# A two-layer hybrid encoder on one core: plain token tiles in the last output projection, and the memory keys' fetch and the gates' exchange moved

## The chip, the core and the metric

The kernel runs on one core of one Trainium2 chip. The metric is the device time of one execution in microseconds. The core has a matrix engine (TensorE, PE in the profile, with its weight loads as PEld), a vector engine (VectorE, DVE), an activation engine (ScalarE, ACT), GpSimd (POOL) and a queue engine (SyncE, SP). Each runs its own list of instructions in order; semaphores hold an instruction until what it needs is done. Transfers are issued by SP and POOL and carried by sixteen DMA engines.

## The reference: what is computed

There are 512 tokens of width 2048 and two layers, all in float32. A layer normalises its input, multiplies it with one input projection of 4,928 columns, and splits the result into latents for attention, three blocks for a short gated convolution, queries for the memory, and gates:

```python
h = rmsnorm(x, pre_norm_g[l])
z = h @ w_in[l]
q_lat, kv_lat, k_pe, gb, gc, xin, q_mem, gate = split_cols(z)
# group A: latent attention, 8 heads of 192, rotary part of 64, softmax over all 512 tokens
# group B: gb * conv3(gc * xin) along the tokens
# group C: attention of 4 heads of 128 into 256 memory tokens
y = jnp.concatenate([a_out, c_out, m_out], axis=-1) * jax.nn.silu(gate)
o = y @ w_o[l]
x = x + rmsnorm(o, post_norm_g[l])
```

The rotary tables come from the token positions, and the memory tokens are normalised and projected to keys and values in every layer.

## The kernel before

**Products.** TensorE multiplies float32 numbers as two parts each: a high part rounded to `fp32r` and the low rest. Each product is three matmuls (`mm3`, L272 to L274): high by high, high by low, low by high. ScalarE makes the high part of a weight tile (L189, `wh`), VectorE the low part (L190, `wl`). The large products go by Strassen's scheme: seven products `P1` to `P7` of half-size blocks instead of eight, in a `group` of passes. The function `ended` adds finished products into the output tiles, and sums of weight blocks are formed by accumulating transfers that POOL issues (L146, `wr`).

**Stages of a layer.** The input projection runs as five groups. The fifth makes the attention's gates `ga0` and `ga1`; between its steps stand turns of the latents and of the memory queries (`more`). Then `mixer` runs: the rotary part of the queries (`q_rope_steps`: products `qr` on TensorE, then a rotation on VectorE, L1067 to L1077, with a table `tab` that is fetched from DRAM, split and written back to DRAM and reloaded as `QR`), then sixteen steps of the four memory heads, then eight attention heads with the first pass of the output projection mixed in. A step of a head is a score product `sc`, its negated row maximum `nm` on VectorE (L1182), an exponential on ScalarE (L1185), a reciprocal `rec` (L1187), a scaling (L1188), a transposition `ptp` on TensorE (L1198), its split into `PT` (L277, L278), and a product `o` with the values, which is multiplied by the gates in `y` (L1213). Last comes `out_proj`: two groups of 1024 columns, each finished token tile squared and summed (L1346), multiplied with the gain (L1350) and added to the residual `xr` (L1395).

**Token order.** The host gives x in an order in which each tile of 128 tokens takes 32 from each quarter of a 128-token block; 32 x 32 transposes on VectorE (L933) and sixteen small transfers (`exchange`, L941) then bring the gates into rows by channel, `y`, with tokens in plain order. The output projection takes its left operand from `y`. With `Left(False, True)` (argument `apart`) the splits reorder the tokens back into the host's tiles, so that the result's tile t holds tokens 32t to 32t+31 of each of the four blocks of 128. The final store is therefore a view of four pieces of 32 rows.

**What sets the order.** The program is a list of steps. TensorE, SP and POOL follow it as written; what a step defers (`pr.defer`) is issued as room comes. VectorE and ScalarE are ordered by a scheduler with its own estimate of when data arrive. Tiles come from pools with a fixed number of buffers: 8 `raw`, 19 `slabs`, 8 PSUM banks. The last group of the last layer keeps the weights of its last product in tiles of their own (`hold`: `T4h` and `T4l`) and runs it as one step, one token half after the other.

Of the kernel before, what the change touches and what calls it, by code (L numbers as in the profile page):

```python
# [12 lines left out]
P = 128  # L13
# [3 lines left out]
NT = S // P  # L17
# [68 lines left out]
class Program:  # L86
# [23 lines left out]
    def add(self, fn, units=(), room=0.0, ahead=None):  # L110

        self.steps.append((list(units), fn, room, self.ahead if ahead is None else ahead))
# [115 lines left out]
def encoder(tc, x, xt, mem, memt, positions, columns, w_in, q_norm_g, w_uq, w_qr, kv_norm_g, w_ukv,  # L228
# [3 lines left out]
    nc = tc.nc  # L232
    depth = w_in.shape[0]
# [15 lines left out]
    add = pr.add  # L249
# [11 lines left out]
    def slab(name, dt=F32):  # L261
        return slabs.tile([P, D], dt, tag="slab", name=nm(name))
# [680 lines left out]
    def gate_rows(k, name, C):  # L943
        def f():
            pr.until(lambda: C.get((name, "turned")) == NT)
            exchange(y_slab(k), C[name])
        return f
# [314 lines left out]
    def mixer(l, C, pair2, tail):  # L1262

        add(tables_fetch)
        add(mem_fetch)
        (p0, rotate0, fetch0), (p1, rotate1, fetch1) = (q_rope_steps(l, g) for g in range(2))
        add(gate_rows(1, "ga1", C))
        put(p0)
        add(gate_rows(0, "ga0", C))
        put(rotate0)  # L1270
        sts = [{} for _ in range(4)]
        qkv = qkv_steps(l, 0, sts[0])
        qkv[0] += (0.0, 1)
        qkv[2] += (0.0, 0)
        put(qkv[:1])
        its = [it for i in range(4) for it in mem_head(i)]
        m = len(its)
        between = {k: [s] for k, s in zip((2, 5, 8, 10, 12), qkv[1:])}
        between.setdefault(6, []).append((fetch0, []))
        between[m - 2] = [(lambda: pr.prep_next(), [])]  # L1280
        for pair in range(4):
            for i in range(2):
                its += mla_head(2 * pair + i, sts[pair])
            nxt = tail if pair == 3 else spread(8, qkv_steps(l, pair + 1, sts[pair + 1]))
            if pair == 0:
                nxt = dict(zip((-1, 1, 3, 4, 6, 7), nxt_steps(nxt)))
            if pair == 2:
                nxt.update(pair2)
            for k, v in nxt.items():
                between.setdefault(m + 8 * pair + k, []).extend(v)  # L1290
        late = [(4, (tables_fetch, [])), (5, p1[0]), (6, p1[1])] + list(zip((6, 7, 8, 9), rotate1)) + [(11, (fetch1, []))]
        if l + 1 < depth:
            late += zip((12, 14, 16, 17, 18, 19, 20, 21), mem_turned_steps(l + 1))
        for k, s in late:
            between.setdefault(m + k, []).append(s)
        pipeline(its, between, m)


    def y_half(k, h):
        return G["ys"][k].rearrange("q c (p k) -> q (c p) k", k=P)[:, :, 64 * h:64 * h + 64]  # L1300

    def out_proj(l):
        last = l == depth - 1
        st = {"n": [0] * NT, "og": {}, "ssq": {}}

        def og(t):
            if t not in st["og"]:
                st["og"][t] = slab("og")
                st["ssq"][t] = small(4, f"ssqo{t}")
            return st["og"][t]  # L1310

        def gains(g):
            def f():
                for j in range(2):
                    st["g", g, j] = scrap("g2")
                    (nc.sync if g else nc.gpsimd).dma_start(st["g", g, j], post_norm_g[l, (2 * g + j) * 512:(2 * g + j + 1) * 512]
                                        .partition_broadcast(P))
            return f

        def block(g):  # L1320
            def f(h, j, c):
                r = h * 1024 + c * 256
                k = (2 * g + j) * 512
                return w_o[l, r:r + 256, k:k + 512].rearrange("(a p) c -> p a c", p=P)
            return f

        def slot(g):
            return lambda i, j, tt: og(2 * i + tt)[:, (2 * g + j) * 512:(2 * g + j + 1) * 512]

        def factor(t):  # L1330
            if last and t == NT - 1:
                st["r", t] = rsqrt_mean(st["ssq"][t][:, 2:3], D, more=st["pre"], on=nc.vector)
            else:
                tot = small(1, "tot2")
                nc.vector.tensor_reduce(tot, st["ssq"][t], axis=AX.X, op=ALU.add)
                st["r", t] = rsqrt_mean(tot, D, on=nc.vector)

        def fin(g):
            def f(i, j, tt, ps=None):
                t, k = 2 * i + tt, 2 * g + j  # L1340
                cs = slice(k * 512, (k + 1) * 512)

                def scale():
                    o = st["og"][t][:, cs]
                    src = o if ps is None else ps
                    nc.scalar.activation(G["junk"], src, AF.Square, accum_out=st["ssq"][t][:, k:k + 1])  # L1346
                    st["n"][t] += 1
                    if st["n"][t] == 4:
                        factor(t)
                    nc.vector.tensor_tensor(o, src, st["g", g, j], op=ALU.mult)  # L1350
                    if last and t == NT - 1 and st["n"][t] == 3:
                        sums = st["ssq"][t]
                        pre = st["pre"] = small(1, "pre")
                        nc.vector.tensor_reduce(pre, sums[:, :2], axis=AX.X, op=ALU.add)
                        nc.vector.tensor_tensor(pre, pre, sums[:, 3:], op=ALU.add)
                        nc.vector.tensor_scalar(pre, pre, 1.0 / D, EPS, op0=ALU.mult, op1=ALU.add)
                    if st["n"][t] == 4:
                        residual(l, st, t)
                if ps is None:
                    pr.defer(0.7, scale)  # L1360
                else:
                    if last and g == 1:
                        pr.until(lambda: st["n"][t] == 3)
                    scale()
            return f

        def fetch(t):
            def f():
                st.setdefault("x", {})[t] = slab("xr")
                nc.gpsimd.dma_start(st["x"][t], G["src"][t * P:(t + 1) * P, :])  # L1370
            return f

        hold_n = [0]

        def hold():
            if hold_n[0] % 2 == 0:
                st["hold"] = slab("T4h", F32R), slab("T4l", F32R)
            k = hold_n[0] % 2
            hold_n[0] += 1
            return tuple(t[:, k * 1024:(k + 1) * 1024] for t in st["hold"])  # L1380

        g0 = group(G["left"], ("o", l, 0), 512, block(0), slot(0), SECOND, fin(0), direct=fin(0))
        g1 = group(G["left"], ("o", l, 1), 512, block(1), slot(1), LATE, fin(1), hold if last else None,
                   direct=fin(1))
        return g0, g1, gains, fetch

    def residual(l, st, t):
# [4 lines left out]
        def part(c, n=1024):  # L1392
            cs = slice(c, c + n)
            xt = st["x"][t]
            nc.vector.scalar_tensor_tensor(xt[:, cs], og[:, cs], st["r", t], xt[:, cs], op0=ALU.mult, op1=ALU.add)  # L1395
            if last:
                nc.sync.dma_start(out[0].rearrange("(p t j) c -> t p j c", t=NT, j=32)[t][:, :, cs], xt[:, cs])
            else:
                nc.gpsimd.dma_start(G["dst"][rows, cs], xt[:, cs])

# [35 lines left out]
    def put(*passes):  # L1436
        for steps in passes:
            for s in steps:
                add(*s)

    def weave(steps, extra, every, n=1):

        out, extra = [], list(extra)
        for k, s in enumerate(steps):
            out.append(s)
            if (k + 1) % every == 0:
                out += extra[:n]
                extra = extra[n:]
        return out + extra
# [10 lines left out]
    for l in range(depth):  # L1460
# [128 lines left out]
        put(g4[13:16])  # L1589
        lat = [latent_turn(l, "cq", j) for j in range(4)] + [latent_turn(l, "ckv", j) for j in range(2)] + [k_rope_turn]  # L1590
        more = [(f, []) for f in lat + [qm_turn(j, C) for j in range(4)]]
        put(weave(g4[16:], more, 2, 2))
        G["left"] = Y = Left(False, True)
        g0, g1, gains, fetch = out_proj(l)

        def low(p):
            return lambda: G["left"].split("A12", p, y_half(2 + p, 0))

        def use_y(Y=Y):
            G["left"] = Y  # L1600

        def sums(p):
            def f():
                a11, a12, a21, a22 = (y_half(k, h) for h in range(2) for k in (p, 2 + p))
                left = G["left"]
                pr.defer(1.2, lambda: left.split("A11", p, a11))
                pr.defer(1.2, lambda: left.split("A22", p, a22))
                combine(left, p, a11, a12, a21, a22)
            return f
# [66 lines left out]
```

## Time and profile before

| what | us |
|---|---|
| median of 3 runs | 1497.22 (1497.14 to 1498.55) |
| profiled execution, its own time | 1496.37 |
| its span, first to last instruction | 1494.5 |
| TensorE busy | 1453.4 (97%) |
| VectorE busy | 1096.8 (73%) |
| ScalarE busy | 871.7 (58%) |
| POOL busy | 270.0 (18%) |
| mean granted TensorE clock | 0.988 |

All times in views of the profile count from the span's start. A row of the timeline has start, duration, engine, line and operation, the tile written `<-` the tiles read, a count where equal rows are merged, and in brackets the idle time just before it with the instruction that ended it. Matmuls overlap: one of 128x512 is listed with 0.39 us, though the next starts 0.23 us later. A DMA row has 16 engines as its whole: a share of 25% is four engines' worth.

### The profile page before, as it was taken

The page shows a single profiled execution, that of the slowest core. Times are in us where ns is not written, and L with a number is a line of the kernel's source. Part 1 is how long each engine was busy: PE and PEld are TensorE (multiplying, and loading weights), DVE is VectorE, ACT ScalarE, POOL GpSimd, SP SyncE. Part 2 cuts the span into 40 slices and gives each one's busy share as a digit, 9 for nine tenths or more (in the row PEclk, how much of TensorE's full clock was granted, in tenths as well). Part 3 has the DMA queues.
Part 4 walks back from the last instruction along what each step waited for, and adds up shares of the span by engine and source line. Part 5 has one row for each costly group of instructions (what it writes and reads, how often), then busy time and mean ns, then how long its engine had stood idle before and what let it go on. Part 6 is the DMA issues. An engine that isn't in the chain of part 4 may idle for free.

```text
span 1494.5 us, 19452 instructions
## 1 busy us (share of the span) xinstructions
PE 1453.4 (97%) x7104; PEld 1239.8 (83%) x7104; DVE 1096.8 (73%) x1461; ACT 871.7 (58%) x1328; POOL 270.0 (18%) x276
## 2 busy tenths in 40 slices
PE   9999999999999999999999999999999999999991
PEld 8887888898878888888898888889988788888881
DVE  5899676957668788878979566766677776877872
ACT  7855345446568787554886334544555767865540
POOL 0031303032201100312201431121131100023010
PEclk9999999999999999999999999999999999999995
DMA  9999979697976462996978999787988915249562
GB/s 358 403 267 217 220 200 178 157 214 203 233 202 147 120 232 74 169 253 159 326 261 256 222 244 215 180 180 169 222 202 199 240 63 118 67 100 188 177 175 93
DMA packets 156348, 295.21 MB, mean 198 GB/s; under 512 B 11292, under 2 KB 46620, under 8 KB 152412
## 3 DMA queue, kind: packets, MB, share of 16 engines
q0 software_dynamic: 56576, 129.51, 43.0%
q1 hardware_dynamic: 99676, 164.45, 34.8%
q8 instruction: 56, 0.92, 0.3%
q14 instruction: 40, 0.33, 0.1%
HBM read 266.01 MB, written 21.63 MB: 192 GB/s over the span
## 4 chain that ended last, share of the span: by engine, by line
PE 94%; DMA 2%; ACT 1%; DVE 1%; SPq 0%; issue 0%; POOLq 0%; DVEq 0%; ACTq 0%
PE P L272 23%; PE P L273 23%; PE P L274 23%; PE ptp L1198 2%; PE o L273 1%; PE o L272 1%; PE o L274 1%; PE sc L274 1%; PE sc L272 1%; PE sc L273 1%; PE tps L915 1%; PE sc L1179 1%; PE qps L272 1%; PE qps L274 1%; PE qps L273 1%; PE sc L1180 1%
## 5 line engine op out<-in xcount | busy, mean ns | idle before, releaser
L190 DVE TENSOR_TENSOR wl<-wr,wh 128x1024 fp32r<-128x1024 f32 (+2 forms) x436 | 515.8, 1187 | 264.1 <-ACT wh L189 260.4
L189 ACT CAST wh<-wr 128x1024 fp32r<-128x1024 f32 (+2 forms) x436 | 444.6, 1023 | 442.6 <-PE P L274 342.3
L272 PE MATMUL P<-wh,S 128*128 128x512 f32 (+1 forms) x896 | 345.1, 385 | 0.0
L273 PE MATMUL P<-wl,S 128*128 128x512 f32 (+1 forms) x896 | 343.7, 384 | 0.0
L274 PE MATMUL P<-wh,S 128*128 128x512 f32 (+1 forms) x896 | 343.2, 383 | 0.0
L272 PE MATMUL P<-wh,A 128*128 128x512 f32 (+1 forms) x656 | 253.0, 386 | 0.0
L273 PE MATMUL P<-wl,A 128*128 128x512 f32 (+1 forms) x656 | 251.8, 384 | 1.1 <-DVE wl L190 1.1
L274 PE MATMUL P<-wh,A 128*128 128x512 f32 (+1 forms) x656 | 251.5, 383 | 0.0
L146 POOL DMA_DIRECT2D wr<-in_w_in_dram x132 | 158.3, 1200 | 444.1 <-DVE wl L190 264.0
L274 PEld LDWEIGHTS P<-wh,S 128*128 128x128 f32 x896 | 168.2, 188 | 30.5
L273 PEld LDWEIGHTS P<-wl,S 128*128 128x128 f32 x896 | 168.2, 188 | 29.5
L272 PEld LDWEIGHTS P<-wh,S 128*128 128x128 f32 x896 | 168.1, 188 | 29.5
L273 PEld LDWEIGHTS P<-wl,A 128*128 128x128 f32 x656 | 123.2, 188 | 23.4 <-DVE wl L190 1.9
L274 PEld LDWEIGHTS P<-wh,A 128*128 128x128 f32 x656 | 123.1, 188 | 22.4
L272 PEld LDWEIGHTS P<-wh,A 128*128 128x128 f32 x656 | 123.1, 188 | 21.7 <-ACT og L586 0.2
L146 POOL DMA_DIRECT2D wr<-in_w_o_dram x40 | 48.4, 1248 | 298.0 <-DVE wl L190 292.9
L1185 ACT ACTIVATE P<-sc,nm 128x512 f32<-128x512 f32 (+1 forms) x96 | 59.4, 619 | 34.9 <-DVE nm L1182 34.5
L1188 ACT ACTIVATE P<-P,rec 128x512 f32<-128x512 f32 (+1 forms) x96 | 62.2, 656 | 5.9 <-DVE rec L1187 5.8
L1182 DVE TENSOR_REDUCE nm<-sc 128x1 f32<-128x512 f32 (+1 forms) x96 | 56.8, 595 | 11.8 <-PE sc L274 6.3
L1198 PE MATMUL ptp<-identr,P 128*128 128x128 f32 x320 | 46.9, 275 | 0.8 <-ACT P L1188 0.8
L178 DVE TENSOR_TENSOR wr<-wr,wr 128x1024 f32<-128x1024 f32 (+1 forms) x36 | 42.2, 1175 | 5.6 <-DMA wr<-in_w_in_dram 5.1
L1198 PEld LDWEIGHTS ptp<-identr,P 128*128 128x128 f32 x320 | 38.5, 142 | 7.4 <-ACT P L1188 1.3
(318 smaller groups left out, 2077.0 us busy)
## 6 DMA issues: line engine op xcount, KB each, us to landing
wr<-in_w_in_dram SPq DMA_DIRECT2D x128, 512.0 KB
wr<-in_w_in_dram POOLq DMA_DIRECT2D x108, 512.0 KB, 7.5
wr<-in_w_o_dram SPq DMA_DIRECT2D x48, 512.0 KB
wr<-in_w_o_dram POOLq DMA_DIRECT2D x40, 512.0 KB, 7.2
wr<-in_w_in_dram SPq DMA_DIRECT2D x32, 416.0 KB
wr<-in_w_in_dram POOLq DMA_DIRECT2D x24, 416.0 KB, 5.9
wr<-in_w_mk_dram SPq DMA_DIRECT2D x15, 512.0 KB
wr<-in_w_mv_dram SPq DMA_DIRECT2D x15, 512.0 KB
```

What stands on the lines that cost most here:

```text
L146: engine.dma_start(dst, src, **kw)
L178: nc.vector.tensor_tensor(tiles[a], tiles[a], tiles[b], op=ALU.add)
L189: pin(nc.scalar.copy(hi[:, h], src[:, h]))
L190: pin(nc.vector.tensor_tensor(lo[:, h], src[:, h], hi[:, h].bitcast(F32), op=ALU.subtract))
L272: nc.tensor.matmul(ps, ah, bh, start=first, stop=False, **kw)
L273: nc.tensor.matmul(ps, ah, bl, start=False, stop=False, **kw)
L274: nc.tensor.matmul(ps, al, bh, start=False, stop=last, **kw)
L915: nc.tensor.transpose(ps[:, t * P:(t + 1) * P], v[:, 4 * j:4 * j + 4].rearrange("p g j -> p (g j)") if len(v.shape) == 3 else v[:, j * P:( ...
L1182: nc.vector.tensor_reduce(nmax, ps, axis=AX.X, op=ALU.max, negate=True)
L1185: nc.scalar.activation(pt, ps, AF.Exp, bias=nmax, accum_out=tot)
L1188: nc.scalar.activation(pt, pt, AF.Copy, scale=rec)
L1198: nc.tensor.transpose(ps[:, k * P:(k + 1) * P], pt[:, k * P:(k + 1) * P], G["ident"])
```

## The change

There are three edits.

In the last layer the output projection no longer reorders its tokens. `Left` is made with `apart` false, `y_half` gives columns 256h to 256h+255 of each channel block as they lie, and the splits are plain. The result's tile t then holds tokens 128t to 128t+127; the residual for it is collected from the tiled DRAM buffer by four transfers of 32 rows each instead of one of 128, and the store goes to 128 consecutive rows.

In both layers `mem_fetch`, which reloads the memory keys `Km` and values `Vm` (1 MB each) from DRAM, is moved from the start of `mixer` to just before the last two entries of the projection's list, the last weight step and the last turn of the memory queries. It now stands ahead of `tables_fetch`.

In both layers the two exchanges of gates are moved from around the `qr` products to steps 2 (`ga0`) and 12 (`ga1`) of the memory heads.

```diff
     def mixer(l, C, pair2, tail):
         add(tables_fetch)
-        add(mem_fetch)
         (p0, rotate0, fetch0), (p1, rotate1, fetch1) = (q_rope_steps(l, g) for g in range(2))
-        add(gate_rows(1, "ga1", C))
-        put(p0)
-        add(gate_rows(0, "ga0", C))
-        put(rotate0)
+        put(p0, rotate0)
...
         between = {k: [s] for k, s in zip((2, 5, 8, 10, 12), qkv[1:])}
+        between.setdefault(2, []).append((gate_rows(0, "ga0", C), []))
         between.setdefault(6, []).append((fetch0, []))
+        between.setdefault(12, []).append((gate_rows(1, "ga1", C), []))
...
-    def y_half(k, h):
+    def y_half(l, k, h):
+        if l == depth - 1:
+            return G["ys"][k][:, :, 256 * h:256 * h + 256]
         return G["ys"][k].rearrange("q c (p k) -> q (c p) k", k=P)[:, :, 64 * h:64 * h + 64]
...
         def fetch(t):
             def f():
-                st.setdefault("x", {})[t] = slab("xr")
-                nc.gpsimd.dma_start(st["x"][t], G["src"][t * P:(t + 1) * P, :])
+                x = st.setdefault("x", {})[t] = slab("xr")
+                if last:
+                    for i in range(NT):
+                        nc.gpsimd.dma_start(x[32 * i:32 * i + 32], G["src"][P * i + 32 * t:P * i + 32 * t + 32, :])
+                else:
+                    nc.gpsimd.dma_start(x, G["src"][t * P:(t + 1) * P, :])
...
             if last:
-                nc.sync.dma_start(out[0].rearrange("(p t j) c -> t p j c", t=NT, j=32)[t][:, :, cs], xt[:, cs])
+                nc.sync.dma_start(out[0][rows, cs], xt[:, cs])
...
-        put(weave(g4[16:], more, 2, 2))
-        G["left"] = Y = Left(False, True)
+        put(weave(g4[16:], more, 2, 2)[:-2])
+        add(mem_fetch)
+        put(weave(g4[16:], more, 2, 2)[-2:])
+        G["left"] = Y = Left(False, l + 1 < depth)
```

The list of TensorE's instructions is the same before and after. Three other lists move where the prediction looks.

ScalarE at the end of the last layer, before (the product P7 has two token halves, `P_1182` and `P_1183`; `T4h` are the high parts of the last product's weights):

```order
L189 CAST wh_12752<-B_1184_12445 128x1024
L189 CAST T4h_12756<-wr_12256 128x1024
L189 CAST T4h_12756<-wr_12274 128x1024
L189 CAST T4h_12776<-wr_12292 128x1024
L189 CAST T4h_12776<-wr_12310 128x1024
L586 COPY og_11668<-P_1182_12415 128x512
L586 COPY og_11679<-P_1183_12416 128x512
L1346 ACTIVATE junk,ssqo_1123_11669<-og_11668 128x512
```

The same place on ScalarE now:

```order
L189 CAST wh_12764<-B_1184_12445 128x1024
L586 COPY og_11668<-P_1182_12415 128x512
L1346 ACTIVATE junk,ssqo_1123_11669<-og_11668 128x512
L586 COPY og_11679<-P_1183_12416 128x512
L189 CAST T4h_12768<-wr_12256 128x1024
L189 CAST T4h_12768<-wr_12274 128x1024
L189 CAST T4h_12788<-wr_12292 128x1024
L189 CAST T4h_12788<-wr_12310 128x1024
```

VectorE at that place now, from its last `wl` on (`T4l` are the low parts of the same weights):

```order
L190 TENSOR_TENSOR wl_12765<-B_1184_12445,wh_12764 128x1024
L587 SCALAR_TENSOR_TENSOR og_11668<-og_11668 128x512
L1350 TENSOR_TENSOR og_11668<-og_11668,g_1186_12466 128x512
L587 SCALAR_TENSOR_TENSOR og_11679<-og_11679 128x512
L1399 SCALAR_TENSOR_TENSOR xr_12553<-og_11666,r_12748,xr_12553 128x1024
L190 TENSOR_TENSOR T4l_12769<-wr_12256,T4h_12768 128x1024
L190 TENSOR_TENSOR T4l_12769<-wr_12274,T4h_12768 128x1024
L190 TENSOR_TENSOR T4l_12789<-wr_12292,T4h_12788 128x1024
L1399 SCALAR_TENSOR_TENSOR xr_12553<-og_11666,r_12748,xr_12553 128x1024
L190 TENSOR_TENSOR T4l_12789<-wr_12310,T4h_12788 128x1024
```

Both copies of P7 and a square now stand ahead of the four casts; in before the casts stood ahead of them, and the four `T4l` stood ahead of both L587.

VectorE at the start of the memory heads of layer 1, before (`rm` and `qr` belong to the rotation, `nm` are the maxima of the memory heads):

```order
L190 TENSOR_TENSOR wl_10142<-wr_9950,wh_10141 128x1024
L190 TENSOR_TENSOR wl_10545<-wr_9968,wh_10544 128x1024
L1182 TENSOR_REDUCE nm_10222<-sc_10218 128x1
L1182 TENSOR_REDUCE nm_10234<-sc_10230 128x1
L1182 TENSOR_REDUCE nm_10246<-sc_10242 128x1
L1187 RECIPROCAL rec_10227<-tot_10225 128x1
L1187 RECIPROCAL rec_10239<-tot_10237 128x1
L1182 TENSOR_REDUCE nm_10273<-sc_10269 128x1
L1187 RECIPROCAL rec_10251<-tot_10249 128x1
L1067 TENSOR_TENSOR rm_10188<-qr_10145,tab_10115 128x1024
```

The same place now:

```order
L190 TENSOR_TENSOR wl_10125<-wr_9950,wh_10124 128x1024
L1067 TENSOR_TENSOR rm_10154<-qr_10128,tab_10119 128x1024
L1071 TENSOR_TENSOR qr_10128<-qr_10141,tab_10119 128x512
L1072 TENSOR_TENSOR qr_10141<-qr_10141,tab_10119 128x512
L1077 TENSOR_TENSOR rm_10154<-rm_10154,qr_10128 128x512
L1076 TENSOR_TENSOR rm_10154<-rm_10154,qr_10141 128x512
L190 TENSOR_TENSOR wl_10545<-wr_9968,wh_10544 128x1024
L278 TENSOR_TENSOR Q_10168<-qps_10169,Q_10168 128x512
L278 TENSOR_TENSOR rm_10154<-rm_10154,qrh_10160 128x1024
L1182 TENSOR_REDUCE nm_10188<-sc_10184 128x1
L1182 TENSOR_REDUCE nm_10200<-sc_10196 128x1
L1182 TENSOR_REDUCE nm_10212<-sc_10208 128x1
```

The whole rotation has moved ahead of the first maximum; it stood behind the fourth.

SP's last stores, before (the sizes are those of the side that is written):

```order
L1397 DMA out_dram<-xr_12553 4x32x1024 x2
L1397 DMA out_dram<-xr_12607 4x32x1024 x2
L1397 DMA out_dram<-xr_12661 4x32x1024 x2
L1397 DMA out_dram<-xr_12750 4x32x256 x2
L1397 DMA out_dram<-xr_12750 4x32x512 x3
```

The same stores now:

```order
L1401 DMA out_dram<-xr_12553 128x1024 x2
L1401 DMA out_dram<-xr_12610 128x1024 x2
L1401 DMA out_dram<-xr_12667 128x1024 x2
L1401 DMA out_dram<-xr_12759 128x256 x2
L1401 DMA out_dram<-xr_12759 128x512 x3
```

Their order and their bytes stay; the shape of each view is another.

More of the change, by code (lines that the diff above doesn't have):

```diff
@@ L1591, in encoder, with low, sums @@
         more = [(f, []) for f in lat + [qm_turn(j, C) for j in range(4)]]
-        put(weave(g4[16:], more, 2, 2))
-        G["left"] = Y = Left(False, True)
+        put(weave(g4[16:], more, 2, 2)[:-2])
+        add(mem_fetch)
+        put(weave(g4[16:], more, 2, 2)[-2:])
+        G["left"] = Y = Left(False, l + 1 < depth)
         g0, g1, gains, fetch = out_proj(l)
-        def low(p):
-            return lambda: G["left"].split("A12", p, y_half(2 + p, 0))
+        def low(p, l=l):
+            return lambda: G["left"].split("A12", p, y_half(l, 2 + p, 0))
         def use_y(Y=Y):
             G["left"] = Y
-        def sums(p):
+        def sums(p, l=l):
             def f():
-                a11, a12, a21, a22 = (y_half(k, h) for h in range(2) for k in (p, 2 + p))
+                a11, a12, a21, a22 = (y_half(l, k, h) for h in range(2) for k in (p, 2 + p))
                 left = G["left"]
```

## The prediction

> **What bounds the kernel now.** I read the busy time of each engine by stage first (columns: stretch and its length in us, then busy us of PE, PEld, DVE, ACT, POOL with instruction counts, granted TensorE clock, DMA share, GB/s).
>
> ```profile
> 0.00:445.00 445.00, 441.91 (x2131) 379.11 (x2132) 329.87 (x436) 249.28 (x326) 88.83 (x87) 1.00 0.93 239
> 445.00:460.00 15.00, 12.47 (x74) 10.81 (x73) 13.74 (x34) 11.91 (x34) 3.68 (x6) 0.89 0.76 185
> 460.00:1173.00 713.00, 713.00 (x3500) 609.80 (x3499) 522.75 (x655) 424.53 (x639) 138.74 (x140) 1.00 0.81 203
> 1173.00:1188.00 15.00, 11.88 (x67) 9.91 (x66) 13.12 (x32) 11.03 (x32) 3.68 (x6) 0.89 0.82 206
> 1188.00:1462.00 274.00, 274.00 (x1341) 230.15 (x1340) 213.63 (x298) 174.29 (x298) 34.51 (x36) 1.00 0.53 130
> 1462.00:1494.50 32.50, 0.15 (x1) 0.00 (x0) 3.68 (x7) 0.69 (x2) 0.54 (x1) 0.53 0.24 91
> ```
>
> TensorE sets the time nearly everywhere: it is never idle from 460 to 1173 and from 1188 to 1462. It loses 2.5 us in the first memory heads, 3.1 us in the second, and then stands still for the last 32 us. The change touches just these three places, so I looked at each. The end first: the last pieces of the chain of waits, then the DMA queues from 1440 to the end and from 1462.4 to 1492.8.
>
> ```profile
> 1461.92 0.24 PE P L274
> ...
> 1464.79 1.99 DVE xr L1395 x3
> ```
> ```profile
> q1 hardware_dynamic: 1452, 4.19, 19.6%
> ```
> ```profile
> GB/s 102 108 102 102 108 102 108 108 108 102 108 102 102 108 102 108 108 108 102 108 102 81 70 62 75 34 75 97 101 100 105 100 105 100 105 100 105 100 67 19
> DMA packets 1127, 2.90 MB, mean 95 GB/s; under 512 B 36, under 2 KB 292, under 8 KB 1127
> ...
> q1 hardware_dynamic: 1127, 2.90, 25.0%
> ```
>
> The last result is computed at 1466.8 (1464.79 + 1.99). Of the 4.19 MB that the hardware queue carries, 2.90 MB are still to be written after 1462.4, and they go at a flat 100 to 108 GB/s until about 1492.8, on 25.0% of the sixteen DMA engines: four. The end is bound by four engines, not by computing.
>
> **Term 1, the output stores.** The store changes from 4x32 rows of a scattered view to 128 plain rows. Nearest row: the store of the layer before has the new form (128 partitions to 128 rows), from the other queue. In 717 to 755 it ran among weight loads:
>
> ```profile
> DMA packets 4078, 12.29 MB, mean 323 GB/s; under 512 B 303, under 2 KB 303, under 8 KB 3632
> ...
> xs<-xr POOLq DMA_DIRECT2D x8, 512.0 KB, 6.6
> ```
>
> So 128-row transfers fill the engines to 323 GB/s, and a 512 KB store lands 6.6 us after issue in that crowd. The first issue of the program shows the delay from SyncE's issue to the first bytes (GB/s in slices of 0.1 us from 0 to 4):
>
> ```profile
> 0.73 0.40 SPq L305 DMA_DIRECT2D cols<-in_columns_dram  x1
> ```
> ```profile
> GB/s 0 0 0 0 0 0 0 0 0 0 0 0 0 0 0 0 0 35 116 148 120 28 106 184 184 225 246 287 246 143 102 82 143 123 225 307 369 348 328 266
> ```
>
> That is 1.0 us. After the change the last store is 256 KB: some 0.5 us behind the stores queued just ahead of it, 1.0 us to the first bytes, 0.8 us at 323 GB/s, and the 1.7 us that the program needs from the last byte (1492.8) to the end of the span: 4.0 us after the last result, where it was 27.7. **Term 1 is -23.7 us.** Bounds: -24.7 with no queueing and 400 GB/s, -19.5 if the last store needs the whole 6.6 us to land.
>
> The Trainium skill ("DMA: Bandwidth & Descriptors", the section on why a DMA increments its semaphore by 16) says that a transfer is split over the largest number of engines up to 16 that divides the slowest dimension of both sides: 4 for the old view, as the 25.0% agrees, and 16 for the new. By its rule term 1 keeps this size.
>
> **Term 2, the last products.** The diff says nothing of it, but the order of ScalarE and VectorE follows the scheduler's view of when data arrive, and sixteen fetches stand where four did. The four casts of the last weights (T4h, L189) now stand behind both copies of the product before (L586), and their low parts (T4l) behind those. Rows of before:
>
> ```profile
> 1444.10 3.89 ACT L189 CAST T4h<-wr 128x1024 fp32r<-128x1024 f32 x4
> ...
> 1449.94 0.59 ACT L586 COPY og<-P 128x512 f32<-128x512 f32 x1 [1.95 <-PE P L274]
> ...
> 1451.30 0.59 ACT L586 COPY og<-P 128x512 f32<-128x512 f32 x1 [0.77 <-PE P L274]
> ...
> 1453.38 0.63 ACT L1346 ACTIVATE junk<-og 128x512 bf16<-128x512 f32 x1 [1.49 <-DVE og L587]
> ```
> ```profile
> 1444.59 1.28 DVE L1395 SCALAR_TENSOR_TENSOR xr<-og,r,xr 128x1024 f32<-128x1024 f32 x1 [0.40 <-POOL r L284]
> ...
> 1446.93 3.49 DVE L190 TENSOR_TENSOR T4l<-wr,T4h 128x1024 fp32r<-128x1024 f32 x3
> ...
> 1451.11 0.39 PE L272 MATMUL P<-T4h,A 128*128 128x512 f32 x1
> ...
> 1451.53 1.22 DVE L190 TENSOR_TENSOR T4l<-wr,T4h 128x1024 fp32r<-128x1024 f32 x1
> ...
> 1452.67 1.28 DVE L587 SCALAR_TENSOR_TENSOR og<-og 128x512 f32<-128x512 f32 x2
> ```
>
> In before the casts are done at 1448, three us ahead of TensorE, which needs the first at 1451.1. Now ScalarE waits for the first copy at 1449.94 and the new order runs thus: copy to 1450.5; L587 (0.64) to 1451.2; square to 1451.85; second copy to 1452.4; first T4h cast to 1453.4, the fourth by 1456.3. VectorE: the product with the gain after the square (0.68) to 1452.5, second L587 to 1453.1, the residual (1.28) to 1454.4, then three T4l at 1.16 each: 1455.5, 1456.7, 1457.9; another residual to 1459.1; the fourth T4l at 1460.3. TensorE starts one product at 1453.4 and can start the second only at 1455.5. From 1451.11 to 1462.16 its 48 products take 0.23 us each, so 47 take 10.8 us from 1455.5; at the fourth quarter, due at 1459.6, it waits 0.7 us more. End 1467.0: 4.8 us later. What waits behind is everything after L274: squares, factor, residual, last store.
>
> A pause of 4.3 us also costs clock. After TensorE's pause of 2.29 us that ends at 1177.91 (row in term 3) the granted clock was 0.50:
>
> ```profile
> 1178.00:1179.00 1.00, 1.00 (x3) 0.81 (x4) 1.00 (x3) 0.76 (x2) 0.00 (x0) 0.50 0.64 123
> ```
>
> The two stretches above at 0.89 mean 15 x 0.11 / 0.5 = 3.3 us at half clock. That loses at most 1.7 us, of which 0.7 us falls into the wait for the fourth T4l: I take 1.0. **Term 2 is +5.8 us**; bounds +4.1 (a copy or residual overlapping more than I let it, full clock) and +7.5 (two such slow spells).
>
> The Trainium skill ("TensorE: Matmul & The Clock Gate", part 1) has the clock halved after an idle window of about 3.4 us on a free-running grid, until a busy one. It speaks against this change; the 3.3 us agrees, and the sum by it is the same but for where the grid falls.
>
> **Term 3, the memory heads.** Rows of layer 1 (layer 0 looks alike):
>
> ```profile
> 1163.18 1.23 DVE L190 TENSOR_TENSOR wl<-wr,wh 128x1024 fp32r<-128x1024 f32 x1
> ...
> 1170.11 1.15 DVE L1182 TENSOR_REDUCE nm<-sc 128x1 f32<-128x256 f32 x3 [0.99 <-PE sc L274]
> ...
> 1174.34 1.21 DVE L1067 TENSOR_TENSOR rm<-qr,tab 128x1024 f32<-128x1024 f32 x1
> ...
> 1175.86 0.69 DVE L1071 TENSOR_TENSOR qr<-qr,tab 128x512 f32<-128x512 f32 x1
> ...
> 1178.24 1.28 DVE L278 TENSOR_TENSOR Q<-qps,Q 128x512 fp32r<-128x512 f32 x2
> 1179.44 1.22 DVE L278 TENSOR_TENSOR rm<-rm,qrh 128x1024 fp32r<-128x1024 f32 x1
> ```
> ```profile
> 1166.61 0.39 PE L274 MATMUL qr<-cqH,wl 128*128 128x512 f32 x1
> ...
> 1173.73 0.38 PE L1198 MATMUL ptp<-identr,P 128*128 128x128 f32 x2
> ...
> 1177.91 0.80 PE L272 MATMUL kps<-ckv,wh 128*128 128x512 f32 x1 [2.29 <-ACT P L1185]
> ```
> ```profile
> 1157.48 0.60 POOL L1046 DMA_DIRECT2D tab<-tabd  x1 [24.82 <-DVE wl L190]
> ```
> ```profile
> tab<-tabd POOLq DMA_DIRECT2D x4, 512.0 KB, 5.4
> ```
>
> In before the rotation of the queries (L1067 to L1076, 1.21 + four at 0.6 to 0.69) sits on VectorE between the maxima of the memory heads. Meanwhile no exponential can run, no PSUM bank comes free, and TensorE waits 2.29 us. In the changed order the rotation stands ahead of the first maximum, where VectorE was idle. It needs the rotary table: issued at 1157.48, landed about 1162.9; fetching the keys and values earlier does not delay it, since POOL stood free from 1132.7 (1157.48 - 24.82). L1067 then runs 1164.4 to 1165.5; after the last qr product (1167.0) the other four to 1169.4; wl to 1170.6; Q to 1171.2; the low part of rm, behind ScalarE's cast, to 1172.4. The maxima come at 1172.4 instead of 1170.1, the reciprocal waits for the fourth (1174.3), and the first transposition (ptp) starts at 1174.9 instead of 1173.73: a new pause of 1.2 us, and walking on by the same durations two of 0.4 and 0.3. So 1.9 us per layer, too short for a clock drop. Removed are 3.1 us idle in layer 1 and 2.5 in layer 0, and in each about 1.5 us of slow clock (half of the 3.3, less what fell into idle time): 8.6 - 3.8 = 4.8, and a little for the tails of matmuls that the view counts as busy. **Term 3 is -5 us**; bounds -8.5 (no new pause) and 0 (the new pauses as long as the old).
>
> **At nothing.** Rows for the fetch of the residual's first tile, for one exchange of gates, and for the casts of weights over the whole run:
>
> ```profile
> 1419.50 1.09 POOL L1370 DMA_DIRECT2D xr<-xs  x1
> ```
> ```profile
> 1174.12 11.98 SPq L941 DMA_DIRECT2D y<-ga  x16
> ```
> ```profile
> L189 ACT CAST wh<-wr 128x1024 fp32r<-128x1024 f32 (+2 forms) x436 | 444.6, 1023 | 442.6 <-PE P L274 342.3
> ```
>
> The splits lose the 32-wide blocks but keep 128x1024 per instruction, and VectorE and ScalarE have room in 1188 to 1462. A fetch in four pieces costs POOL at most 3.3 us more a tile (three more issues of 1.09); the 25 us from this issue to the first use (1444.6) hide it, and without them it would be 3.3 us. An exchange holds SyncE for 12 us; queued behind the two there are now only loads for the output projection, and the gates are wanted first by the MLA heads, after all sixteen memory steps; uncovered it would be those 12 us. The 2 MB of keys and values move to the free stretch of POOL after 1132.7, among the last weights of the projection. There too the casts mostly wait for TensorE to free their buffers (342 of 443 us idle), not for data; if not, 2 MB at 323 GB/s would delay them by 6.5 us.
>
> **The sum.** 1494.5 - 23.7 + 5.8 - 5.0 = 1471.6 us span. The profiled execution took 1496.37, 1.9 more than its span, and lies 0.85 under the median of the runs: 1471.6 + 1.9 + 0.85 = **1474 us**, 1.5% faster.
>
> **The rivals.** (a) The memory heads gain nothing, since the new pauses replace the old: 1479. For it: ScalarE is busy 11 of those 15 us. Against: the 2.29 us wait has its cause on VectorE, and that moves. 0.12. (b) The last products do not stall, as real data come early and ScalarE is not held: 1468. Against: an engine runs in its order, and the copy cannot precede 1449.94. 0.06. (c) The stores stay at 105 GB/s, because SyncE's queue writes no faster: then the stream again sets the end, and it starts with the first residual, now at 1454.4 - 5 = 1449.4 instead of 1445.9 (1444.59 + 1.28): 3.5 us later, time 1501, slower than before. This decides below 4.19 MB / 18.2 us = 230 GB/s (from the first residual to the last, 1466.8 + 5.8 - 5). Against: 323 GB/s above. 0.04.
>
> **How the numbers follow.** The forecast has 0.78, with a range of its own of 1470 to 1478. The range of 8 in 10 takes in (a) and (b): 1467 to 1481. A measurement of this kernel tells about 0.2% (3 us) from no change; only (c) lies above 1497 at all, and at the edge of that: faster 0.96, same 0.02, slower 0.02.
>
> **What would show it.** Right: out_dram stores on near all engines, span ending about 4 us after the last xr; a wait of PE for T4h and then T4l, 2 and 2 us, with a spell at 0.50 clock behind it; no wait of kps for ScalarE, clock 1.00 in both memory stages. Wrong: a flat 105 GB/s at the end; the casts of T4h ahead of L586; the maxima of the memory heads early, or waiting for tab or Km.

## The result, and the profile after

| | before | changed | forecast |
|---|---|---|---|
| median of the runs, us | 1497.18 (1495.92 to 1498.55) | 1473.51 (1472.93 to 1474.58) | 1474 |
| ratio, 95% interval | 1 | 0.9843 (0.9825 to 0.986) | 0.985 |
| span of the profiled execution, us | 1494.5 | 1471.2 | 1471.6 |

Where the time went, term by term. "Memory heads" is the time between the same two matmuls of both traces around each head stage (from the 2,000th to the 2,500th of 7,104, and from the 5,500th to the 6,000th): 96.90 to 94.46 us and 97.41 to 94.43. "Last product" runs from the last matmul ahead of the T4h product to that product's last one: 10.88 to 17.41. "After the last residual" runs from the end of the last xr to the end of the span: 27.7 to 3.9.

| term, us | forecast | measured |
|---|---|---|
| stores: after the last residual | -23.7 | -23.8 |
| last product | +5.8 | +6.5 |
| memory heads, both layers | -5.0 | -5.4 |
| the rest, most of it in the first 225 us | 0 | -0.6 |
| span | -22.9 | -23.3 |

Busy time by stage in the changed kernel (columns as before the change: stretch and length, busy us of PE, PEld, DVE, ACT, POOL with instruction counts, granted clock, DMA share, GB/s):

```profile
445.00:460.00 15.00, 13.91 (x92) 12.25 (x93) 10.75 (x35) 13.90 (x46) 2.20 (x4) 1.00 1.09 221
460.00:1170.00 710.00, 710.00 (x3477) 606.99 (x3476) 525.09 (x653) 421.09 (x625) 139.31 (x142) 1.00 0.80 203
1170.00:1185.00 15.00, 13.75 (x92) 11.92 (x91) 11.18 (x36) 13.79 (x47) 2.87 (x5) 1.00 1.09 262
1185.00:1445.00 260.00, 260.00 (x1268) 218.17 (x1266) 196.22 (x273) 165.04 (x278) 40.11 (x47) 1.00 0.56 130
1445.00:1462.60 17.60, 13.94 (x50) 10.52 (x48) 15.04 (x19) 6.39 (x11) 0.97 (x1) 0.81 0.36 137
1462.60:1471.20 8.60, 0.09 (x1) 0.00 (x0) 3.68 (x7) 0.69 (x2) 0.54 (x1) 0.80 0.60 222
```

Both memory stages run at clock 1.00 now, with 1.1 and 1.25 us idle where 2.5 and 3.1 stood. A new loss has come in at 1445 to 1462.6: 3.7 us idle and a clock of 0.81. The last stretch is 8.6 us where 32.5 stood. TensorE's waits of the changed kernel (us in total, times, longest) name them:

```profile
PE ptp L1198 <- ACT P L1188: 2.3, 2, 1.1
PE P L272 <- ACT T4h L189: 2.2, 1, 2.2
PE P L273 <- DVE T4l L190: 1.4, 1, 1.4
```

The wait of kps for ScalarE, 4.2 us in two before, is gone. The stores of the changed kernel, in the stretch from 1464.5 to the end, first as GB/s in 40 slices and the share of the sixteen engines, then as issues with KB and median us to landing:

```profile
GB/s 391 25 0 0 0 0 0 79 318 324 165 336 306 49 342 391 391 330 208 404 367 355 379 379 367 330 294 110 49 24 12 0 0 0 0 0 0 0 0 0
...
out_dram<-xr SPq DMA_DIRECT2D x3, 256.0 KB, 2.7
out_dram<-xr SPq DMA_DIRECT2D x2, 128.0 KB, 1.9
```

They go in bursts of about 300 to 400 GB/s as results come, and no longer at a flat rate. Next, ScalarE and VectorE around the pause, from the timeline of the changed kernel:

```profile
1443.95 0.59 ACT L586 COPY og<-P 128x512 f32<-128x512 f32 x1 [5.75 <-PE P L274]
...
1445.92 0.57 ACT L586 COPY og<-P 128x512 f32<-128x512 f32 x1
1446.39 3.88 ACT L189 CAST T4h<-wr 128x1024 fp32r<-128x1024 f32 x4
```
```profile
1447.26 1.28 DVE L1399 SCALAR_TENSOR_TENSOR xr<-og,r,xr 128x1024 f32<-128x1024 f32 x1
1448.46 3.48 DVE L190 TENSOR_TENSOR T4l<-wr,T4h 128x1024 fp32r<-128x1024 f32 x3
...
1465.32 1.99 DVE xr L1399 x3
```

ScalarE is idle for 5.75 us, waiting for the product whose copy stands ahead of the casts. (The last row is from the chain of waits: the last residual ends at 1467.3.) Last, VectorE and TensorE at the memory heads of layer 1: the rotation (L1067) now starts 8 us ahead of the first maximum (L1182), and the first transposition `ptp` waits 1.13 us.

```profile
1161.52 1.23 DVE L1067 TENSOR_TENSOR rm<-qr,tab 128x1024 f32<-128x1024 f32 x1
...
1169.49 1.08 DVE L1182 TENSOR_REDUCE nm<-sc 128x1 f32<-128x256 f32 x3
```
```profile
1172.04 0.44 PE L1198 MATMUL ptp<-identr,P 128*128 128x128 f32 x2 [1.13 <-ACT P L1188]
```

### The profile page after: what moved, and what is told of

The parts are those of the page before. It is cut to its first block, busy times and chain, and to the rows that moved or that the text cites. A ratio compares the mean times of both kernels' runs of the same rounds, so it can differ in the third digit from the quotient of the medians.

```text
span 1471.2 us, 19483 instructions
## 1 busy us (share of the span) xinstructions
PE 1454.2 (99%) x7104; PEld 1239.1 (84%) x7104; DVE 1096.7 (75%) x1461; ACT 870.4 (59%) x1328; POOL 275.2 (19%) x288
## 4 chain that ended last, share of the span: by engine, by line
PE 88%; DMA 4%; DVE 4%; ACT 2%; issue 1%; SPq 0%; POOL 0%; POOLq 0%; DVEq 0%; ACTq 0%
PE P L273 22%; PE P L274 22%; PE P L272 22%; DMA wr<-in_w_in_dram 2%; PE ptp L1198 2%; PE o L273 1%; PE o L274 1%; PE o L272 1%; PE sc L272 1%; DVE wl L190 1%; PE sc L274 1%; PE sc L273 1%; PE tps L915 1%; PE sc L1179 1%; PE qps L272 1%
## 5 line engine op out<-in xcount | busy, mean ns | idle before, releaser
L273 PEld LDWEIGHTS P<-wl,A 128*128 128x128 f32 x656 | 123.2, 188 | 22.9 <-DVE wl L190 1.4
L1182 DVE TENSOR_REDUCE nm<-sc 128x1 f32<-128x512 f32 (+1 forms) x96 | 56.8, 595 | 14.3 <-PE sc L1180 9.1
```

Of the source, the lines that this page charges most:

```text
L273: nc.tensor.matmul(ps, ah, bl, start=False, stop=False, **kw)
L1182: nc.vector.tensor_reduce(nmax, ps, axis=AX.X, op=ALU.max, negate=True)
```

## The experiments

Each kernel was timed beside the kernel before on the same chip (whose medians there were 1495.9 to 1496.9), with four or five runs each; the three store views were run once each.

### The two halves of the change, apart

The kernel with the first edit alone is the changed one with these lines back:

```diff
-        put(p0, rotate0)
+        add(mem_fetch)          # after tables_fetch
+        add(gate_rows(1, "ga1", C))
+        put(p0)
+        add(gate_rows(0, "ga0", C))
+        put(rotate0)
...
-        between.setdefault(2, []).append((gate_rows(0, "ga0", C), []))
-        between.setdefault(12, []).append((gate_rows(1, "ga1", C), []))
...
-        put(weave(g4[16:], more, 2, 2)[:-2])
-        add(mem_fetch)
-        put(weave(g4[16:], more, 2, 2)[-2:])
+        put(weave(g4[16:], more, 2, 2))
```

> The first edit alone (plain token tiles, plain stores, four-piece fetches; gates and keys where they were before). Theory, by the three terms as the changed trace has them (stores -23.7, the pause before the held weights +6.5, memory heads -5.4): the memory heads pause as before, so 1473.5 + 5.4 = 1479 us; the pause for T4h and T4l stays. Rival: the gain at the memory heads is a by-product of the new stores and fetches, through the order that the scheduler finds: then 1473.5.

Measured: 1479.51 us, ratio 0.9891 (0.9876 to 0.9905). Its trace has the old waits at the heads and the new ones at the end:

```profile
PE kps L272 <- ACT P L1185: 4.2, 2, 2.3
...
PE P L272 <- ACT T4h L189: 2.2, 1, 2.2
PE P L273 <- DVE T4l L190: 1.7, 1, 1.7
```

The head stages take 96.84 and 97.20 us as before the change. So the gain there does not come from the new tiles, and the pause at the end does.

The other half takes the output back to the old tiles:

```diff
-                nc.sync.dma_start(out[0][rows, cs], xt[:, cs])
+                nc.sync.dma_start(out[0].rearrange("(p t j) c -> t p j c", t=NT, j=32)[t][:, :, cs], xt[:, cs])
...
-                if last:
-                    for i in range(NT):
-                        nc.gpsimd.dma_start(x[32 * i:32 * i + 32], G["src"][P * i + 32 * t:P * i + 32 * t + 32, :])
-                else:
-                    nc.gpsimd.dma_start(x, G["src"][t * P:(t + 1) * P, :])
+                nc.gpsimd.dma_start(x, G["src"][t * P:(t + 1) * P, :])
```

(with `y_half` and `Left` as before).

> The two moves at the memory heads alone (gates and keys moved, output tiles, fetches and stores as before). Theory: -5.4 at the heads, and the stream of stores on four engines starts 5.4 us earlier and still ends the span: 1497.2 - 5.4 = 1491.8 us, no pause for T4h. Rival: something other than the start of the stream fixes its end: 1497. Rival: the pause for T4h comes from the moves at the heads: then the last matmul ends some 6 us later than by the theory, though the stream still sets the end.

Measured: 1490.59 us, ratio 0.9966 (0.9953 to 0.9979). The head stages take 94.46 and 94.42 us, the last product 10.88, and from 1457 to 1487 the stores keep the old rate on four engines:

```profile
GB/s 104 109 109 104 104 104 104 109 109 104 104 104 104 109 104 104 104 104 109 109 104 98 87 55 78 53 31 91 100 101 100 104 115 98 104 104 101 104 98 57
DMA packets 1127, 2.92 MB, mean 97 GB/s; under 512 B 34, under 2 KB 290, under 8 KB 1126
...
q1 hardware_dynamic: 1126, 2.91, 25.5%
```

The heads are worth 5.3 us of their own (1495.9 - 1490.6), also where the stream sets the end, since it starts that much earlier. The halves add up: -16.4 and -5.3 make -21.7, and the whole change measured -23.7 on another chip. Each of the three has an interval of 2 to 3 us to either side, so the 2 us between them are not resolved.

### The number of engines behind a store

The changed kernel, with only the view of its stores exchanged (the rows of the output land in other places than they should; bytes, order and issue stay):

```diff
-                nc.sync.dma_start(out[0][rows, cs], xt[:, cs])
+                nc.sync.dma_start(out[0].rearrange("(p t j) c -> t p j c", t=NT, j=32)[t][:, :, cs], xt[:, cs])
```

and the same with j=16 (blocks of 16 rows, eight of them) and j=8 (sixteen blocks of 8 rows).

> The changed kernel with its stores in the old 4x32 view (the rows land in the old kernel's places, which are wrong for plain tiles; amounts and times of issue stay). Theory (the view sets the number of engines): four engines, a flat 105 GB/s, 4.19 MB take 40 us from 1449.6 to 1489.5, span 1491, time 1493.5. Rival (the rate was low because of the old product order or of reads of the old tiles): 1473.5.

> The same with a view of 8x16 rows (rows misplaced). Theory: eight engines, 200 to 210 GB/s; the last 1.0 MB, issued from 1465 on, takes 5 us instead of 2.7: span 1473, time 1475.5. Rival (blocks of rows that lie apart are slow, however many): smaller blocks are slower than 4x32, 1493 or more.

> The same with a view of 16x8 rows (rows misplaced). Theory: sixteen engines, 400 GB/s in bursts, as the plain rows: span 1471, time 1473.5. Rival (blocks that lie apart are slow): 1493 or more.

Measured: 1498.44, 1479.88 and 1475.63 us. Rate and share of the engines from 1470 to 1490 with 4x32 and from 1462 to 1475 with 8x16, where the queue was full, and from 1466 to 1473 with 16x8, where it was not full throughout (the row DMA is the busy share of the sixteen engines in tenths, in 40 slices):

```profile
DMA packets 795, 2.05 MB, mean 103 GB/s; under 512 B 22, under 2 KB 278, under 8 KB 794
...
q1 hardware_dynamic: 794, 2.04, 25.9%
```
```profile
DMA packets 997, 2.46 MB, mean 189 GB/s; under 512 B 59, under 2 KB 315, under 8 KB 996
...
q1 hardware_dynamic: 996, 2.45, 50.7%
```
```profile
DMA  9899999632699379747789757999979899751000
GB/s 304 328 398 445 374 421 421 258 117 70 152 199 293 105 164 240 246 158 152 152 211 293 211 199 258 316 234 293 281 246 281 246 257 304 269 199 59 0 0 0
...
q1 hardware_dynamic: 884, 1.59, 73.0%
...
out_dram<-xr SPq DMA_DIRECT2D x3, 256.0 KB, 3.3
```

A quarter, a half, and in the bursts of the third view nine tenths or more of the engines (73.0% over the whole stretch), by the outer count of the view: 4, 8, 16. From the end of the last residual to the end of the span it is 27.3, 10.7 and 5.0 us, against 3.9 with plain rows. So the count of blocks sets the rate; that the rows lie apart costs little (256 KB land in 3.3 us instead of 2.7). The 4x32 and 8x16 views came out 5 and 4 us above the expectation, which had the stream run at its full rate from the first residual on. In the trace of the 4x32 view it ran at only 20 to 75 GB/s in its first 6 us (1451 to 1457), with data waiting; why is open. With eight engines 4.19 MB at 189 GB/s already take 22 us, longer than the 18 in which the results come, so these stores are behind as well.

### The pause ahead of the last product

First, one fetch for each tile of the residual in place of four:

```diff
-                if last:
-                    for i in range(NT):
-                        nc.gpsimd.dma_start(x[32 * i:32 * i + 32], G["src"][P * i + 32 * t:P * i + 32 * t + 32, :])
-                else:
-                    nc.gpsimd.dma_start(x, G["src"][t * P:(t + 1) * P, :])
+                src = G["src"].rearrange("(p t j) c -> t p j c", t=NT, j=32)[t] if last else G["src"][t * P:(t + 1) * P, :]
+                nc.gpsimd.dma_start(x, src)
```

> The changed kernel with the residual of the last layer fetched by one transfer per tile in the 4x32 view instead of four pieces; same rows, same result. The order of ScalarE has the T4h casts ahead of the two copies again. Theory: the pause of 2.2 and 1.4 us and the slow clock behind it go, 6.5 us: 1467 us. Rival: the pause stays because data are late (the 4x32 view loads a tile on four engines, 5 us for 512 KB at 105 GB/s, and the residual waits for it): 1473.5 or more.

Measured: 1473.91 us, ratio 0.9853 (0.9836 to 0.9869): the rival. The first half of the theory held: TensorE waits for neither T4h nor T4l, and the last product takes 11.29 us instead of 17.41. But the time comes back as a wait of the residual, in VectorE's timeline and in the fetches from 1440 to 1463:

```profile
1440.31 2.94 ACT L189 CAST T4h<-wr 128x1024 fp32r<-128x1024 f32 x3
```
```profile
1462.06 1.28 DVE L1396 SCALAR_TENSOR_TENSOR xr<-og,r,xr 128x1024 f32<-128x1024 f32 x1 [6.40 <-DMA xr<-xs]
```
```profile
xr<-xs POOLq DMA_DIRECT2D x2, 1024.0 KB, 20.9
```

A tile is 1 MB, not the 512 KB that I had put into the expectation, and two of them, fetched in the 4x32 view beside weights and stores, took some 21 us each; the plain fetch of a tile in the kernel before landed in 8.9 us (median of two, from 1418 to 1433). They were also issued late. The third fetch stands on GpSimd's queue behind the last load of weights, which went out only at 1438.01:

```profile
1438.01 1.22 POOL L146 DMA_DIRECT2D wr<-in_w_o_dram  x1 [14.74 <-DVE og L579]
```

So the third fetch was issued at 1440.37, where the changed kernel issues the third tile's pieces from 1428.19. Whether that load waited for VectorE, as the view has it, or for the first fetch, which landed within 0.3 us of the same time, is not shown. So the casts' place was the cause of the pause, but this cure moved the wait.

The second cure keeps the four pieces and moves them to the queue of SyncE:

```diff
-                        nc.gpsimd.dma_start(x[32 * i:32 * i + 32], G["src"][P * i + 32 * t:P * i + 32 * t + 32, :])
+                        nc.sync.dma_start(x[32 * i:32 * i + 32], G["src"][P * i + 32 * t:P * i + 32 * t + 32, :])
```

> The changed kernel with the sixteen 32-row fetches of the residual issued by SyncE instead of GpSimd; same rows, same result. SyncE issues nothing between 1385.6 and 1448.6 in the changed trace. The order of ScalarE has the T4h casts ahead of the copies again, as in the kernel with one fetch per tile, but the pieces of 32 rows spread over sixteen engines. Theory: the last product takes 10.9 us as before the change and not 17.4, nothing waits for the residual: 1473.5 - 6.5 = 1467 us. Rival: the residual is late again, this time behind the stores on the same queue: 1472 or more.

Measured: 1467.17 us (1466.69 to 1468.36), ratio 0.9805 (0.9792 to 0.9819), below the changed kernel's 0.9843 (0.9825 to 0.986) as well. SyncE's queue and the casts in its timeline, and the busy times over the last product:

```profile
1387.31 0.37 SPq L146 DMA_DIRECT2D wr<-in_w_o_dram  x1
1387.72 28.73 SPq L1372 DMA_DIRECT2D xr<-xs  x16
1443.29 19.95 SPq L1401 DMA_DIRECT2D out_dram<-xr  x11
```
```profile
1430.22 1.05 ACT L189 CAST T4h<-wr 128x1024 fp32r<-128x1024 f32 x1
...
1435.45 1.06 ACT L189 CAST T4h<-wr 128x1024 fp32r<-128x1024 f32 x1
...
1446.05 0.59 ACT L586 COPY og<-P 128x512 f32<-128x512 f32 x1 [5.74 <-PE P L274]
```
```profile
1446.50:1458.30 11.80, 11.75 (x52) 9.38 (x50) 8.52 (x14) 2.77 (x8) 0.96 (x1) 1.00 0.40 156
```

The last product takes 10.88 us, to the hundredth what it took before the change, at clock 1.00. The same sixteen transfers on the other queue take the whole of term 2 away. On GpSimd's queue of the changed kernel the last two loads of weights stand behind pieces of the residual:

```profile
1413.51 2.51 POOL L1372 DMA_DIRECT2D xr<-xs  x4
1419.07 1.26 POOL L146 DMA_DIRECT2D wr<-in_w_o_dram  x1 [3.05 <-DVE wl L190]
1419.86 2.48 POOL L1372 DMA_DIRECT2D xr<-xs  x4
1427.42 1.27 POOL L146 DMA_DIRECT2D wr<-in_w_o_dram  x1 [5.08 <-DVE wl L190]
```

With the pieces gone from that queue, or fewer, the scheduler places the casts early; which delay it reckons with for those loads no run here shows. The chip itself had issued the last of them by 1428.7, 16 us before the product was due.

Third, what of the 6.5 us is idle and what is clock. Nine matmuls of constants fill TensorE's wait for T4h:

```diff
-        put(g1[3][1:], g1[4])
+        put(g1[3][1:])
+        if l + 1 == depth:
+            add(lambda: warm(9))
+        put(g1[4])
```

> The changed kernel with nine matmuls of constants, which nothing reads, ahead of the last product, in the 2.2 us in which TensorE waits for T4h. What the pause costs beside its idle time: the last product cost 6.5 us more than before, of which 2.2 + 1.4 idle. Theory: the other 2.8 us are the clock at 0.50 from 1447.2 to 1454.1; with TensorE busy up to T4h only the 1.4 us wait for T4l is left, which leaves the clock at 1.00: 1473.5 - 2.8 = 1470.7. Rival: the 1.4 us wait alone still costs the clock: 1472 to 1473.5.

Measured: 1473.67 us, ratio 0.9851 (0.9836 to 0.9865): no gain where 2.8 us were expected. In the one trace the clock did what the theory says:

```profile
1447.00:1449.50 2.50, 2.39 (x11) 1.65 (x9) 1.71 (x4) 2.13 (x5) 0.00 (x0) 1.00 0.20 39
1449.50:1452.00 2.50, 0.69 (x2) 0.38 (x3) 2.50 (x3) 2.50 (x4) 0.00 (x0) 1.00 0.21 85
1452.00:1458.00 6.00, 5.78 (x25) 4.44 (x25) 6.00 (x6) 0.42 (x2) 0.00 (x0) 1.00 0.36 142
```

It stays at 1.00 through a wait of 1.74 us for T4l. The same stretch of the changed kernel, without the filling, lay at half clock for 6.8 us:

```profile
1447.00:1448.00 1.00, 0.51 (x1) 0.29 (x1) 1.00 (x2) 1.00 (x2) 0.00 (x0) 0.62 0.00 0
1448.00:1454.00 6.00, 4.55 (x11) 3.40 (x11) 6.00 (x6) 2.27 (x3) 0.00 (x0) 0.50 0.22 87
1454.00:1462.00 8.00, 8.00 (x36) 6.60 (x36) 6.37 (x11) 1.41 (x4) 0.97 (x1) 1.00 0.50 199
```

But the last product still takes 15.93 us: at full clock TensorE comes sooner to the low parts and waits longer for them (1.74 and 0.22 us, in place of 1.45 and nothing). So of the 6.5 us, 5.0 are the late casts (15.93 - 10.88) and 1.5 the clock; my 2.8 had taken for clock what at full clock turns into waiting. These 1.5 us do not show in the median. In this trace TensorE is 1.75 us later by 225 us than in that of the changed kernel, most of it in waits for the first weights; whether that is chance or comes from the order of the casts, which shifts through the whole program with the nine matmuls, stays open.

### Which move frees the memory heads

The changed kernel with one of the two moves taken back, first the fetch of the keys, then the exchanges of gates:

```diff
         add(tables_fetch)
+        add(mem_fetch)
...
-        put(weave(g4[16:], more, 2, 2)[:-2])
-        add(mem_fetch)
-        put(weave(g4[16:], more, 2, 2)[-2:])
+        put(weave(g4[16:], more, 2, 2))
```

> The changed kernel with the fetch of the memory keys put back after the fetch of the rotary table; the gates stay moved. The order of VectorE and ScalarE at the memory heads is that of the changed kernel. Theory (the order on VectorE is the gain, and it comes with the exchanges of gates; the earlier fetch is worth nothing): 1473.5. Rival (the earlier fetch is what lets the heads start): the 5.4 us are lost, 1479.

```diff
-        put(p0, rotate0)
+        add(gate_rows(1, "ga1", C))
+        put(p0)
+        add(gate_rows(0, "ga0", C))
+        put(rotate0)
...
-        between.setdefault(2, []).append((gate_rows(0, "ga0", C), []))
-        between.setdefault(12, []).append((gate_rows(1, "ga1", C), []))
```

> The changed kernel with the exchanges of gates put back ahead of the memory heads; the early fetch of the keys stays. The rotation is then early as well, but cut by the first maximum, and the second rotated half and its low part stand between maxima. Theory, walked by the durations of the trace: pauses of 1.9 and 0.9 us per layer before the transpositions instead of 1.1: 1473.5 + 2 x 1.5 = 1476.5, to 1479.5 if a pause costs clock. Rival (the exchanges hold something that the heads wait for): the pauses of 2 us of the kernel before come back, 1479.

Measured: 1473.8 us, ratio 0.9845 (0.983 to 0.9859), without the earlier fetch; 1476.95, 0.9869 (0.9853 to 0.9886), without the moved exchanges. The first has head stages of 94.42 and 94.38 us, those of the changed kernel: the moved exchanges, with the order that follows from them, bring the whole gain, and the earlier fetch adds nothing to them. Alone, the earlier fetch is not worthless. The second kernel has head stages of 95.07 and 96.43 us, where the kernel with neither move has 96.84 and 97.20: 2.5 us of the gain, since the rotation is ahead there too (L1067 starts at 1166.85, before the first maximum at 1167.98). So either move brings the rotation forward, and the two gains do not add. The second has these pauses and these stages:

```profile
PE ptp L1198 <- ACT P L1188: 4.9, 4, 1.7
```
```profile
445.00:460.00 15.00, 12.53 (x89) 11.44 (x89) 12.41 (x37) 14.14 (x46) 3.68 (x6) 1.00 0.93 215
1170.00:1185.00 15.00, 12.53 (x71) 10.79 (x71) 11.04 (x32) 11.97 (x37) 3.67 (x6) 0.89 0.88 229
```

Against the changed kernel it loses 0.6 us in layer 0 and 2.0 in layer 1. The idle time is 2.5 us in both, and only in layer 1 the clock fell.

## Why the prediction was right

**What bounds the kernel, and term 1.** The stream on four engines set the end, and a view with 128 rows ends that. The tail after the last residual was worked out as 4.0 us and is 3.9. The Trainium skill ("DMA: Bandwidth & Descriptors", the section on why a DMA increments its semaphore by 16) gives the largest number up to 16 that divides the slowest dimension of both sides as the number of engines; the three store views agree, with shares of 25.9%, 50.7% and, for 16 blocks, nine tenths and more in bursts. Rival (c), stores that stay slow, is what the 4x32 view in the changed kernel builds: 1498 us, where I had worked out 1501. The lower bound of this term was added wrongly: 1.0 + 0.7 + 1.7 us leave -24.3, not -24.7.

**Term 2.** The part that the diff does not tell was in the order of ScalarE and VectorE, and the walk by durations held. The first T4h cast starts 1.3 us after the product was due (1446.39 against 1445.11), worked out as 1.3; the first low part ends 4.6 us after it, worked out as 4.4. The idle part is 5.0 us for 4.8. The clock is the part mis-sized: I gave one spell of 3.3 us, and it was 6.8, which costs 1.5 us for my 1.0. Of the bounds, "two such slow spells" had named it. Whether it is one spell or two looks like chance. Seven of the kernels here have this pause, each with one trace. In three of them (the first edit alone, the 8x16 stores, the changed kernel without the earlier fetch) the mean clock over the 18 us from the last matmul ahead of the T4h product is 0.91, that is 3.2 us at half clock, and their last product takes 16.85 to 17.04 us: about 1.0 more than the 15.93 at full clock, as I had it. In the other four it is 0.81, that is 6.8 us, and 17.41 to 18.22. The Trainium skill ("TensorE: Matmul & The Clock Gate", part 1) has windows of about 3.4 us on a free-running grid; 6.8 us agrees with two of them, and 3.2 with one. The kernel before needed no whole window of idle time: pauses of 1.9 and 2.3 us cost a spell each, and the measurement decides. That pauses of 1.7 and 0.8 us within 2 us cost the clock in one layer and not in the other, in the kernel without the moved exchanges, agrees with a grid as well; no run here shifts the grid on purpose to prove it. Rival (b), no pause, is what the fetch by SyncE builds: 1467.2, where I had worked out 1468.

**Term 3.** The wait of 2.29 us went with the rotation ahead of the maxima, and rival (a) fell: 5.4 us gained, 5.3 with the heads alone. My walk had three new pauses, 1.9 us per layer; the trace has one of 1.1 and almost nothing behind it. By the rows of the two memory stages idle time fell by 3.3 us in all, where I had 5.6 - 3.8 = 1.8. That leaves 2.1 us of the 5.4 for the slow clock, where I had 3.0. The two errors offset each other, so that the term comes out only 0.4 off; that part is luck.

**At nothing.** The fetch of the keys among the last weights cost nothing, and beside the moved exchanges it gave nothing. The exchanges inside the heads cost nothing. The four-piece fetches did not cost GpSimd time that anyone waited for; their whole price was term 2, through the order. The rest of the difference, -0.6 us, lies in the start of the program, where traces of kernels that are alike there differ by up to 2 us.

So the sum is right by its terms and not only by its total: the errors are -0.1, +0.7 and -0.4 us, and -0.6 for the start. The three mechanisms are the ones forecast; what looks like chance is in the second spell of term 2, and luck in the offset within term 3.

## What to carry to other kernels

When the end of a kernel is a flat line of GB/s on a round fraction of the engines, look at the outermost count of the view that is written. Changing only transfers can still change the order of compute where a scheduler sets it; compare the order on each engine before believing that an edit costs nothing, and follow the queue that the new transfers stand in, since the same transfers on an idle queue may be free (here 1473.5 against 1467.2 us). A cure for a late cast is worth its time only if what it makes late instead has room: the single fetch took the pause away and gave it back as a late residual.

## What the runs showed of the hardware that I had not expected

- A fetch of 1 MB in a view of 4x32 rows landed 21 us after its issue beside other traffic, where a plain one in the kernel before landed in 8.9 us and the sixteen pieces of 256 KB of the changed kernel landed in 7.9 us (median; a tile's four are issued within 2.5 us, the slowest took 10.2).
- SyncE was busy longer with a store whose view has blocks: 0.54 us per issue with 16x8 against 0.33 with plain rows (median of eleven).
- Filling a wait of 2.2 us with matmuls left the clock at 1.00 through the next wait of 1.7 us (one trace), and yet gave back only 1.5 us, since the faster product met the same late operands.
- The same pause ahead of the last product cost 3.2 us at half clock in three kernels and 6.8 us in four.
